# A transformer block on one Trainium2 core: softmax rows normalised in pairs, weight roundings of the output projection moved apart, its first sums in other banks

## The chip, the cores and the metric

The kernel runs on one core of a Trainium2 chip. A core has a matrix engine (TensorE, PE in the profile; PEld is its weight load), VectorE (DVE), ScalarE (ACT), GpSimd (POOL) and SyncE (SP), which here only starts transfers. The engines run side by side, each takes its instructions in order, and they wait for each other through semaphores. Matrix products land in PSUM, of which this kernel uses eight banks of 128 x 512 numbers. Transfers between HBM and the core's memory are issued by SP and POOL into queues and carried out by 16 DMA engines. A special kind, the accumulating load, adds what it reads to what already stands in the tile; it is issued by POOL.

The metric is the device time of one execution in microseconds. Times below are of single executions or medians of several.

## The reference

Inputs are x (512 rows of 1024), weights and gains in float32. The parts that matter here:

```python
q = concat([q_nope, rope(q_rope)]) * (MLA_QK_HEAD ** -0.5)     # 8 heads, 96 wide
s = einsum('qhd,thd->hqt', q, k)                                 # 512 x 512 per head
p = softmax(s); y_mla = p @ v                                  # v is 128 wide per head
merged = sigmoid(z_ma) * y_gla + sigmoid(z_mb) * y_mla         # 512 x 1024
h = h + merged @ w_out                                         # 1024 x 1024
m = rmsnorm(h, g_mlp)
h = h + square(relu(m @ w_ff1)) @ w_ff2                        # 1024 x 4096 x 1024
return rmsnorm(h, g_final)
```

Ahead of them stand a norm, the input projections and a gated linear attention that gives y_gla.

## The kernel before, in words

*Precision.* A float32 operand is split into a high half (rounded on ACT, L93, or with a gain L97) and a low half (the difference, on DVE or POOL, L94 and L98). `mm3` then makes each product from three matmuls: high by high (L88), high by low (L89), low by high (L90). "A rounding step" below is one such pair of ACT and DVE instructions.

*Attention.* It starts at 303.85 us of the profiled span. The 8 heads go in 4 pairs. `up_units(pr)` is a generator that, step by step, loads and splits a pair's weights (wq, wk), and makes its queries (uq), keys (uk) and values (uv). A loop `for n in range(38)` goes over 32 steps of 128 query rows: `att_scores` for row block n (three matmuls into a bank `s`; the negated maximum on DVE, L1007; the exponential with its sum `tot` on ACT, L1010; the reciprocal on DVE, L1011; the scaling, on ACT for even blocks, L1015, and on DVE for odd ones, L1013), `att_flip` for block n - 3 (four transposes into a bank `tp`, L1024, and their rounding into `pT`), and `att_values` for block n - 6 (matmuls into `av`). `merge` multiplies a head's values by its gate on DVE (`tb`, L1052) and adds y_gla on POOL (L1055), which gives `mx` and `my` of the pair. `next(units)` hands one step of the next pair's preparation to the loop in each iteration.

*Output projection.* merged @ w_out is made with seven products in place of eight (m = 1, 2, 5, 6, 3, 7, 4), each of a left operand made of sums of merged blocks and a right operand made of blocks of w_out, B11, B12, B21 and B22. `merged_sums` forms the sums `yo` and `zo` (L928 to L931), `split_sum`, `split_first` and `corner` round them (`ghbo`/`glbo`, `ghco`/`glco`, `gao`, `gdo`). The right side stands in tiles `w2_00` to `w2_31`: `load_w2` fills them through SP's queue (four 256 KB loads for a block), `load_onto` adds another block in place through POOL's queue (two loads of 512 KB, L908), `add_w2` adds two blocks on DVE (L912). `split_part` and `split_w2` round half a block or a block into `bo` and product number, as in bo10 and bo11 (128 x 1024 numbers each). The products land in banks `wox`, `wow` and `woz`, and `add_rows` adds them into the rows `h` (L1298).

*Between projection and feed-forward part.* Each row block of h gets its norm: squares with sums on ACT in two halves (L173), mean and power on DVE and POOL (L180, L183), the scaling in halves on DVE (L1314) and ACT (L1315). PE flips the scaled rows `ms` into banks `mb` (L198), `fm.evacuate` rounds them into `mT`, and `proj_begin`/`proj_run` make the first hidden columns f00 and f01 (`early`), then f02 and so on in four quarters.

*Order.* The Tile framework's scheduler places the instructions. `goes_behind` binds one step behind another on chosen engines. From `begun`, which stands ahead of the projection's products, `in_program_order` keeps PE, DVE and ACT in the order of the code; POOL keeps it from `attending` on, the start of the attention loop. SP's queue takes its loads in the order of the code as far as the scheduler leaves it. PSUM banks are of two kinds, "at" and "mm", four each, handed out in turn: scores, flips and some accumulators take "at"; head preparations, values and others "mm". Rounded weights have 4 buffers for each half, staged ones 3.

Of the kernel before, what the change touches and what calls it, by code (L numbers as in the profile page):

```python
# [56 lines left out]
def tile_block(ctx: ExitStack, tc: tile.TileContext, t, out: bass.AP):  # L57
# [128 lines left out]
    class Flipped:  # L186
# [5 lines left out]
        def rows(self, i, xs):  # L192
            half = i // 2
            if half not in self.banks:
                self.banks[half] = [ps("mm", f"{self.name}b{half}{j}") for j in range(4)]
# [703 lines left out]
    def load_w2(qd, x, w=w2):  # L899
        for g, dst in enumerate(block_tiles(x)):  # L900
            for pp_ in range(2):
                nc.sync.dma_start(dst[:, pp_, :], block_rows(w, qd, x, g, pp_))
# [7 lines left out]
    def add_w2(dst, x, y, op):  # L910
        for g in range(NP // 2):
            nc.vector.tensor_tensor(wq[dst][g], wq[x][g], wq[y][g], op=op)  # L912

# [84 lines left out]
    probs, pTs, avs = {}, {}, {}  # L998

    def att_scores(head, qt):  # L1000
# [8 lines left out]
        tot = sm("tot", 1)  # L1009
        nc.scalar.activation(e, acc, AF.Exp, bias=top, accum_out=tot)  # L1010
        nc.vector.reciprocal(tot, tot)  # L1011
        if qt % 2:
            nc.vector.tensor_scalar(e, e, tot, None, op0=ALU.mult)  # L1013
        else:
            nc.scalar.activation(e, e, AF.Copy, scale=tot)  # L1015
        probs[head, qt] = e
# [225 lines left out]
    units = iter(())  # L1242
    attending = traced()
    sums_of = {}
    for n in range(4 * MH + LAG_C):
        if n % 8 == 1 and n // 8 + 1 < MH // 2:
            units = up_units(n // 8 + 1)
        scored = traced()
        if n < 4 * MH:
            att_scores(n // 4, n % 4)  # L1250
        scored = scored, traced()
        next(units, None)
        b = n - LAG_B
        if 0 <= b < 4 * MH:
            flips = traced()
            att_flip(b // 4, b % 4)
            if b == 0:
                gla_turn(GH - 1, (flips, traced()))

        ready = traced()  # L1260
        if n in (17, 25, 31):
            p = (n - 13) // 8
            y, z = sums_of.pop(p)
            split_sum(wo_left[p], y, 5, 6, f"bo{p}", nc.gpsimd)
            split_sum(wo_left[p], z, 7, 3, f"co{p}", nc.gpsimd)
            if p == 1:
                for p in range(2):
                    split_first(wo_left[p], merged[p][0], f"o{p}", nc.gpsimd)
            goes_behind((ready, traced()), scored, SPLITTERS[:1])
        if n == 20:  # L1270
            load_w2(0, B11, w_out)
            load_w2(0, B21, w_out)
        if n == 24:
            wo_right[1] = split_w2(B11, "bo1")
        if n == 27:
            wo_right[2] = split_w2(B21, "bo2")
        if n == 28:
            load_onto(B11, B12, w_out)
        if n == 30:
            load_w2(0, B12, w_out)  # L1280
            load_w2(0, B22, w_out)
        c = n - LAG_C
# [328 lines left out]
```

## Time and profile before

| what | before |
|---|---|
| three runs | 778.02 (median), 777.01, 778.77 us |
| profiled execution | 777.01 us, its span 775.3 us |
| PE busy | 757.8 us, 98% of the span |
| DVE busy | 584.6 us, 75% |
| ACT busy | 452.9 us, 58% |
| POOL busy | 148.9 us, 19% |
| mean DMA rate | 99 GB/s |
| mean granted clock of PE | 0.99 |

The span runs from the first to the last instruction of the profile. The rows of slices cut it into 40 equal parts of 19.4 us; a digit is the busy share in tenths, and PEclk the clock that TensorE was granted, in tenths of full speed. A row of a group reads: line, engine, operation, output and inputs with their shapes, count; busy microseconds and mean nanoseconds of one; the engine's idle time just before them and what ended it. A row of waits reads: what PE was about to do, on which result of which engine it waited, microseconds in total, times, the longest. The chain of waits goes back from a late instruction, at each step to what released it.

### The profile page before, as it was taken

Reading aid. Unit: us, or ns where it says so; the run is one execution under the profiler, and the core shown is the slowest. Engines: PE = TensorE matmul, PEld = TensorE weight load, DVE = VectorE, ACT = ScalarE, POOL = GpSimd, SP = SyncE. Lnnn points to the kernel's source line nnn. Section 1 sums busy time; section 2 is a strip of 40 time slices with the busy share of each in tenths; the row PEclk is TensorE's granted clock in tenths of the full one; section 3 lists DMA queues with packets and bytes.
Section 4 is the critical chain, followed back from the end, with each engine's and each line's share of the span. In section 5 each row is a group of like instructions: output and inputs, shape, how many; then the busy total and the mean of one; then the engine's idle time right before and its main releaser. Section 6 shows DMA issues by size and latency. Waiting matters only on the chain.

```text
span 775.3 us, 10210 instructions
## 1 busy us (share of the span) xinstructions
PE 757.8 (98%) x3744; PEld 640.1 (83%) x3744; DVE 584.6 (75%) x866; ACT 452.9 (58%) x768; POOL 148.9 (19%) x224
## 2 busy tenths in 40 slices
PE   9999999999999999999799899999999999999996
PEld 7888788889888888898687788888888888888885
DVE  7788999666677776989887677965787578848695
ACT  7556667556475546978735675544644465336644
POOL 0810006161533124044741000000000000000014
PEclk9999999999999999999899899999999999999999
DMA  9734201132325324014766231164106510560002
GB/s 313 244 110 135 71 18 29 54 82 55 82 55 135 52 55 106 22 36 142 219 162 187 84 109 55 58 202 120 55 30 188 151 40 27 171 183 0 28 1 108
DMA packets 94945, 77.09 MB, mean 99 GB/s; under 512 B 15312, under 2 KB 74704, under 8 KB 94896
## 3 DMA queue, kind: packets, MB, share of 16 engines
q1 hardware_dynamic: 92752, 72.24, 31.6%
q0 software_dynamic: 1856, 3.93, 2.7%
q8 instruction: 29, 0.48, 0.3%
q10 hardware_dynamic: 288, 0.28, 0.1%
q14 instruction: 20, 0.16, 0.1%
HBM read 72.76 MB, written 2.10 MB: 97 GB/s over the span
## 4 chain that ended last, share of the span: by engine, by line
PE 93%; DVE 4%; issue 1%; ACT 1%; POOL 0%; POOLq 0%; DVEq 0%; ACTq 0%
PE f L89 8%; PE f L90 8%; PE f L88 8%; PE gx L88 4%; PE gx L89 4%; PE gx L90 4%; PE first L326 3%; PE za L88 2%; PE za L89 2%; PE za L90 2%; PE gz L89 2%; PE gz L90 2%; PE gz L88 2%; PE tp L1024 2%; PE zb L88 1%; PE zb L90 1%
## 5 line engine op out<-in xcount | busy, mean ns | idle before, releaser
L1550 POOL DMA_DIRECT2D gfin<-in_g_final x1 | 0.6, 622 | 283.7 <-PE f L90 283.7
L912 DVE TENSOR_TENSOR w<-w,w 128x1024 f32<-128x1024 f32 x34 | 41.1, 1220 | 0.3
L474 POOL COPY v3f<-rrf 128x4 f32<-128x4 f32 x4 | 2.8, 708 | 135.8 <-DVE rrf L457 135.8
L1010 ACT ACTIVATE e<-s,top 128x512 f32<-128x512 f32 x32 | 21.9, 685 | 6.7 <-DVE top L1007 6.1
L1298 DVE TENSOR_TENSOR h<-h,gx 128x512 f32<-128x512 f32 x32 | 21.5, 680 | 1.9 <-PE gx L90 1.8
L1007 DVE TENSOR_REDUCE top<-s 128x1 f32<-128x512 f32 x32 | 21.6, 679 | 1.4 <-PE s L90 1.4
L94 DVE TENSOR_TENSOR pT<-tp,pT 128x512 fp32r<-128x512 f32 x32 | 21.5, 679 | 0.4 <-ACT pT L93 0.2
L93 ACT ACTIVATE pT<-tp 128x512 fp32r<-128x512 f32 x32 | 18.8, 594 | 4.9 <-PE tp L1024 4.9
L88 PE MATMUL av<-pT,v 128*128 128x256 f32 x64 | 19.5, 304 | 1.3 <-ACT pT L93 1.3
L1024 PE MATMUL tp<-ident,e 128*128 128x128 f32 x128 | 20.1, 281 | 0.0
L89 PE MATMUL av<-pT,v 128*128 128x256 f32 x64 | 18.6, 291 | 0.1
L1024 PEld LDWEIGHTS tp<-ident,e 128*128 128x128 f32 x128 | 16.2, 146 | 3.1 <-issue 0.4
L1370 ACT ACTIVATE fa<-f 128x512 f32<-128x512 f32 x32 | 18.5, 577 | 0.0
L90 PE MATMUL av<-pT,v 128*128 128x256 f32 x64 | 18.4, 288 | 0.0
L93 ACT ACTIVATE ghb<-y 128x512 fp32r<-128x512 f32 x16 | 10.1, 632 | 14.0 <-DVE y L859 14.0
L94 DVE TENSOR_TENSOR sc<-sc,sc 128x512 fp32r<-128x512 f32 x16 | 10.9, 690 | 9.5 <-ACT sc L93 9.5
L88 PE MATMUL s<-kbuf,q 96*128 96x512 f32 x32 | 14.5, 453 | 3.2 <-DVE pT L94 3.2
L93 ACT ACTIVATE sc<-sc 128x512 fp32r<-128x512 f32 x16 | 9.3, 596 | 11.5 <-DVE sc L545 11.5
L1055 POOL TENSOR_TENSOR mx<-tb,za 128x256 f32<-128x256 f32 x8 | 6.9, 868 | 40.9 <-DVE tb L1052 40.9
L93 ACT ACTIVATE b_00h<-w 128x1024 fp32r<-128x1024 f32 x7 | 7.4, 1060 | 12.6 <-PE gx L90 6.0
L93 ACT ACTIVATE b_10h<-w 128x1024 fp32r<-128x1024 f32 x7 | 7.4, 1061 | 12.1 <-PE gz L90 6.0
L93 ACT ACTIVATE b_20h<-w 128x1024 fp32r<-128x1024 f32 x7 | 7.4, 1060 | 11.9 <-PE gz L90 6.0
(1639 smaller groups left out, 2940.7 us busy)
## 6 DMA issues: line engine op xcount, KB each, us to landing
w<-in_w_ff SPq DMA_DIRECT2D x64, 256.0 KB, 3.4
grw<-in_w_in SPq DMA_DIRECT2D x8, 512.0 KB, 8.6
gvw<-in_w_in SPq DMA_DIRECT2D x8, 512.0 KB, 4.8
w<-in_w_out SPq DMA_DIRECT2D x16, 256.0 KB, 5.2
w<-in_w_out POOLq DMA_DIRECT2D x6, 512.0 KB, 7.9
x<-in_xt SPq DMA_DIRECT2D x8, 256.0 KB, 5.3
vw<-in_w_first SPq DMA_DIRECT2D x8, 256.0 KB, 5.4
h<-in_x SPq DMA_DIRECT2D x4, 512.0 KB, 10.7
```

Source lines behind the costliest of these rows:

```text
L88: nc.tensor.matmul(acc, lh, rh, start=start, stop=False, skip_group_check=onto)
L89: nc.tensor.matmul(acc, lh, rl, start=False, stop=False, skip_group_check=onto)
L90: nc.tensor.matmul(acc, ll, rh, start=False, stop=stop, skip_group_check=onto)
L93: nc.scalar.activation(hi, src, AF.Copy)
L94: rest.tensor_tensor(lo, src, raw(hi), op=ALU.subtract)
L326: nc.tensor.matmul(f_accs[i], a[:, i * P : (i + 1) * P], b, start=k == 0 and x == 0, stop=k == KD - 1 and x == 2)
L912: nc.vector.tensor_tensor(wq[dst][g], wq[x][g], wq[y][g], op=op)
L1007: nc.vector.tensor_reduce(top, acc, axis=AX.X, op=ALU.max, negate=True)
L1010: nc.scalar.activation(e, acc, AF.Exp, bias=top, accum_out=tot)
L1024: nc.tensor.transpose(tp[:, k * P : (k + 1) * P], e[:, k * P : (k + 1) * P], ident)
L1298: nc.vector.tensor_tensor(hc, hc, acc, op=op)
L1370: nc.scalar.activation(a, acc, AF.Relu)
```

## The change

Seven things change; the diff has them in the order of the code.

1. *Pairs of rows.* The sums of two row blocks stand in one tile of two columns. A new `att_normalise`, called at even n for blocks n - 2 and n - 1, takes one reciprocal for both, scales the even block on ACT and the odd one on DVE. The scores' steps on ACT and DVE are bound behind those of the flip made two iterations earlier.
2. *Head preparations.* The weights of the next pair are loaded and split earlier (ahead of the loop, at n = 6 and n = 14), and the steps are taken only at n % 8 from 2 to 6.
3. *Rounding of products 1 and 2.* A new `streamed` loads half a block of w_out into a staging buffer (two 256 KB loads on SP) and rounds it, at n = 11 and 13 (B11, product 1) and n = 21 and 23 (B21, product 2). Before, whole blocks were loaded at n = 20 and rounded at n = 24 and 27.
4. *Other blocks.* The tiles of B11 and B21 are then filled for products 5, 6 and 4 by loads and accumulating loads between n = 22 and n = 34, and two additions on DVE for product 6 go. Accumulating loads become 10 from 6, loads of w_out 24 from 16.
5. *Sums of the left side.* `yo` and `zo` of a pair are rounded in iterations of their own (18, 26, 32 and 20, 28, 33), the first blocks at 19, 30 and 35.
6. *Banks.* `wox` and the early f00 and f01 go to "mm", `wow` and the flips of the rows to "at".
7. *Products 3, 7 and 4 with the norms.* `normed` is cut into `second_half_square` and `scaled`; product 4's weights are rounded after both upper rows are scaled; product 7's second half, the flips and their evacuation are interleaved; f00 and f01 begin later; the two lower rows are scaled together after product 4.

```diff
@@ -192,7 +192,7 @@
         def rows(self, i, xs):
             half = i // 2
             if half not in self.banks:
-                self.banks[half] = [ps("mm", f"{self.name}b{half}{j}") for j in range(4)]
+                self.banks[half] = [ps("at", f"{self.name}b{half}{j}") for j in range(4)]
             for k in range(KD):
                 at = (k // 4) * 256 + (i % 2) * P
                 nc.tensor.transpose(
@@ -896,10 +896,11 @@
         c = (x % 2) * S
         return w[r : r + P, c : c + S]
 
-    def load_w2(qd, x, w=w2):
+    def load_w2(qd, x, w=w2, block=None):
+
         for g, dst in enumerate(block_tiles(x)):
             for pp_ in range(2):
-                nc.sync.dma_start(dst[:, pp_, :], block_rows(w, qd, x, g, pp_))
+                nc.sync.dma_start(dst[:, pp_, :], block_rows(w, qd, x if block is None else block, g, pp_))
 
@@ -910,6 +911,15 @@
     def add_w2(dst, x, y, op):
         for g in range(NP // 2):
             nc.vector.tensor_tensor(wq[dst][g], wq[x][g], wq[y][g], op=op)
+
+    def streamed(m, x, g):
+
+        wf = stage(2, S, f"bo{m}{g}")
+        for pp_ in range(2):
+            nc.sync.dma_start(wf[:, pp_, :], block_rows(w_out, 0, x, g, pp_))
+        wh, wl = halves(2, S, f"bo{m}{g}")
+        split(wh, wl, wf)
+        wo_right.setdefault(m, []).append((wh, wl))
 
     def split_part(x, g, name):
         wh, wl = halves(2, S, f"{name}{g}")
@@ -995,7 +1005,7 @@
         for i in range(2):
             heads[2 * pr + i] = (qs[i], kbuf[2 * (pr % 2) + i], vs, slice(i * MV, (i + 1) * MV))
 
-    probs, pTs, avs = {}, {}, {}
+    probs, pTs, avs, tots = {}, {}, {}, {}
 
     def att_scores(head, qt):
         q, kb, _, _ = heads[head]
@@ -1006,14 +1016,17 @@
         top = sm("top", 1)
         nc.vector.tensor_reduce(top, acc, axis=AX.X, op=ALU.max, negate=True)
         e = u2(f"e{head}{qt}")
-        tot = sm("tot", 1)
-        nc.scalar.activation(e, acc, AF.Exp, bias=top, accum_out=tot)
+        if qt % 2 == 0:
+            tots[head] = sm("tot", 2)
+        tot = tots[head]
+        nc.scalar.activation(e, acc, AF.Exp, bias=top, accum_out=tot[:, qt % 2 : qt % 2 + 1])
+        probs[head, qt] = e
+
+    def att_normalise(head, qt):
+        tot, a, b = tots[head], probs[head, qt], probs[head, qt + 1]
         nc.vector.reciprocal(tot, tot)
-        if qt % 2:
-            nc.vector.tensor_scalar(e, e, tot, None, op0=ALU.mult)
-        else:
-            nc.scalar.activation(e, e, AF.Copy, scale=tot)
-        probs[head, qt] = e
+        nc.scalar.activation(a, a, AF.Copy, scale=tot[:, 0:1])
+        nc.vector.tensor_scalar(b, b, tot[:, 1:2], None, op0=ALU.mult)
 
     def att_flip(head, qt):
         e = probs.pop((head, qt))
@@ -1239,51 +1252,69 @@
     rs = gla_squares(h, os)
     gla_gated(h, os, rs)
     LAG_B, LAG_C = 3, 6
-    units = iter(())
+    units = up_units(1)
+    next(units)
     attending = traced()
-    sums_of = {}
+    sums_of, flipping = {}, {}
     for n in range(4 * MH + LAG_C):
-        if n % 8 == 1 and n // 8 + 1 < MH // 2:
-            units = up_units(n // 8 + 1)
+        if n % 2 == 0 and 2 <= n <= 4 * MH:
+            att_normalise((n - 2) // 4, (n - 2) % 4)
         scored = traced()
         if n < 4 * MH:
             att_scores(n // 4, n % 4)
+            if n - 2 in flipping:
+                goes_behind((scored, traced()), flipping[n - 2], SPLITTERS)
         scored = scored, traced()
-        next(units, None)
+        if 2 <= n % 8 < 7:
+            next(units, None)
+        if n in (6, 14):
+            units = up_units(n // 8 + 2)
+            next(units)
         b = n - LAG_B
         if 0 <= b < 4 * MH:
             flips = traced()
             att_flip(b // 4, b % 4)
+            flipping[n] = flips, traced()
             if b == 0:
                 gla_turn(GH - 1, (flips, traced()))
 
-        ready = traced()
-        if n in (17, 25, 31):
-            p = (n - 13) // 8
-            y, z = sums_of.pop(p)
-            split_sum(wo_left[p], y, 5, 6, f"bo{p}", nc.gpsimd)
-            split_sum(wo_left[p], z, 7, 3, f"co{p}", nc.gpsimd)
-            if p == 1:
-                for p in range(2):
-                    split_first(wo_left[p], merged[p][0], f"o{p}", nc.gpsimd)
-            goes_behind((ready, traced()), scored, SPLITTERS[:1])
-        if n == 20:
+        extra = traced()
+        for x, at in (("y", (18, 26, 32)), ("z", (20, 28, 33))):
+            if n in at:
+                p = at.index(n)
+                to = (5, 6) if x == "y" else (7, 3)
+                split_sum(wo_left[p], sums_of[p, x], *to, f"{x}o{p}", nc.gpsimd)
+        if n in (19, 30):
+            p = (19, 30).index(n)
+            split_first(wo_left[p], merged[p][0], f"o{p}", nc.gpsimd)
+        if n < 4 * MH:
+            goes_behind((extra, traced()), scored, SPLITTERS[:1])
+        if n == 35:
+            split_first(wo_left[2], merged[2][0], "o2")
+        if n in (11, 13):
+            streamed(1, B11, (n - 11) // 2)
+        if n in (21, 23):
+            streamed(2, B21, (n - 21) // 2)
+        if n == 22:
             load_w2(0, B11, w_out)
-            load_w2(0, B21, w_out)
-        if n == 24:
-            wo_right[1] = split_w2(B11, "bo1")
+        if n == 23:
+            load_w2(0, B21, w_out, B22)
+        if n == 25:
+            load_onto(B11, B12, w_out)
         if n == 27:
-            wo_right[2] = split_w2(B21, "bo2")
+            load_onto(B21, B11, w_out)
         if n == 28:
-            load_onto(B11, B12, w_out)
-        if n == 30:
             load_w2(0, B12, w_out)
             load_w2(0, B22, w_out)
+        if n == 31:
+            load_onto(B21, B12, w_out)
+        if n == 34:
+            load_onto(B12, B22, w_out)
         c = n - LAG_C
         if c >= 0 and c % 2 == 1:
             att_values(c // 4, (c % 4) // 2)
         if c > 0 and c % 8 == 7 and c // 8 < NP - 1:
-            sums_of[c // 8] = merged_sums(c // 8, nc.gpsimd)
+            sums_of[c // 8, "y"], sums_of[c // 8, "z"] = merged_sums(c // 8, nc.gpsimd)
 
     hrow = []
     for i in range(NT):
@@ -1306,21 +1337,17 @@
 
     span = {}
 
-    def normed(i, last_half):
-        at = traced()
+    def second_half_square(i, c):
+        square_half(hrow[i], c, hparts[i], ms_rows[i], False)
+
+    def scaled(i):
         m = ms_rows[i]
-        square_half(hrow[i], last_half, hparts[i], m, False)
         rs = row_rstd(hparts[i])
         nc.vector.tensor_scalar(m[:, 0:S], hrow[i][:, 0:S], rs, None, op0=ALU.mult)
         nc.scalar.activation(m[:, S:D], hrow[i][:, S:D], AF.Copy, scale=rs)
-        span["norm", i] = at, traced()
 
     def flipped(i):
         fm.rows(i, ms_rows[i])
-        if i % 2 == 1:
-            at = traced()
-            fm.evacuate(i // 2)
-            span["evacuate", i // 2] = at, traced()
 
 
     def prep(m, qd):
@@ -1455,9 +1482,9 @@
 
 
     begun = traced()
-    xs_ = [ps("at", f"wox{rb}") for rb in range(2)]
+    xs_ = [ps("mm", f"wox{rb}") for rb in range(2)]
+    ws_ = [ps("at", f"wow{rb}") for rb in range(2)]
     zs_ = [ps("at", f"woz{rb}") for rb in range(2)]
-    ws_ = [ps("mm", f"wow{rb}") for rb in range(2)]
     wo_accs = {2: ws_, 5: zs_, 3: zs_}
 
     def wo_product(m, rbs=range(2), ps_=range(NP)):
@@ -1471,7 +1498,6 @@
                     m in (1, 2, 5) and p == 0, p == NP - 1, m not in (1, 2, 5))
 
     last = NP - 1
-    split_first(wo_left[2], merged[2][0], "o2", nc.vector)
     g_last = split_first(wo_left[last], merged[last][0], f"o{last}", nc.vector, None, slice(0, HT))
     wo_product(1)
     wo_right[5] = [split_part(B11, 0, "bo5")]
@@ -1479,19 +1505,18 @@
     y, z = merged_sums(last, nc.vector)
     split_sum(wo_left[last], y, 5, 6, f"bo{last}")
     wo_right[5].append(split_part(B11, 1, "bo5"))
-    load_onto(B12, B22, w_out)
-    add_w2(B11, B22, B11, ALU.add)
+    load_w2(0, B11)
     for rb in range(2):
         add_rows(rb, 0, xs_[rb])
     wo_product(2)
-    wo_right[6] = [split_part(B11, 0, "bo6")]
+    wo_right[6] = [split_part(B21, 0, "bo6")]
     for rb in range(2):
         add_rows(rb, 0, ws_[rb])
+    wo_right[6].append(split_part(B21, 1, "bo6"))
+    load_onto(B21, B21, w_out)
+    split_sum(wo_left[last], z, 7, 3, f"co{last}")
+    for rb in range(2):
         first_half_square(rb, 0)
-    wo_right[6].append(split_part(B11, 1, "bo6"))
-    load_onto(B11, B21, w_out)
-    load_w2(0, B21)
-    split_sum(wo_left[last], z, 7, 3, f"co{last}")
     wo_product(5)
     wo_right[3] = [split_part(B22, 0, "bo3")]
     for rb in range(2):
@@ -1511,24 +1536,42 @@
     for rb in range(2):
         wo_product(3, (rb,))
         add_rows(rb, 1, zs_[rb])
-        normed(rb, 1)
-        wo_right.setdefault(4, []).append(split_part(B11, rb, "bo4"))
-    load_w2(0, B11)
-    early = [proj_begin(w1, 0, "f00", "at")]
-    for rb in range(2):
-        wo_product(7, (rb,))
-        add_rows(2 + rb, 1, xs_[rb], ALU.subtract)
-        first_half_square(2 + rb, 1)
-        flipped(rb)
-    early.append(proj_begin(w1, P, "f01", "at"))
-    for rb in range(2):
-        wo_product(4, (rb,))
-        add_rows(2 + rb, 0, xs_[rb])
-        normed(2 + rb, 0)
+        second_half_square(rb, 1)
+        scaled(rb)
+    wo_right[4] = split_w2(B21, "bo4")
+    load_w2(0, B21)
+    wo_product(7, (0,))
+    add_rows(2, 1, xs_[0], ALU.subtract)
+    first_half_square(2, 1)
+    flipped(0)
+    wo_product(7, (1,), range(2))
+    flipped(1)
+    at = traced()
+    fm.evacuate(0, range(4))
+    wo_product(7, (1,), range(2, NP))
+    add_rows(3, 1, xs_[1], ALU.subtract)
+    fm.evacuate(0, range(4, KD))
+    first_half_square(3, 1)
+    span["evacuate", 0] = at, traced()
+    early = [proj_begin(w1, 0, "f00", "mm")]
+    wo_product(4, (0,))
+    add_rows(2, 0, xs_[0])
+    second_half_square(2, 0)
+    early.append(proj_begin(w1, P, "f01", "mm"))
+    wo_product(4, (1,))
+    at = traced()
+    add_rows(3, 0, xs_[1])
+    second_half_square(3, 0)
+    for i in (2, 3):
+        scaled(i)
+    span["norm", 3] = at, traced()
     proj_run(early[0], mT, 0)
     proj_run(early[1], mT, 0, range(5))
     flipped(2)
     flipped(3)
+    at = traced()
+    fm.evacuate(1)
+    span["evacuate", 1] = at, traced()
     proj_run(early[1], mT, 0, range(5, KD))
     for k in range(KD):
         for e in early:
```

## The prediction, made before the result was known

> **What bounds it now.** I read the page's slices first (busy tenths and granted clock), then busy time by stretch, then what TensorE (PE) waited for, then the chain of waits.
>
> ```profile
> PE   9999999999999999999799899999999999999996
> ...
> PEclk9999999999999999999899899999999999999999
> ```
>
> PE is busy in nearly every slice. It dips in two places, around 370 and 430 us, and the granted clock dips with it. The change acts between 304 and 452 us, so I cut that stretch at four PE events: the first attention score (303.85), the end of head 5's scores (360.67), the end of the projection's product 1 (397.01), the middle of its product 3 (416.05) and the first whole product of the feed-forward part (451.67).
>
> ```profile
> core 0: us, PE busy (x) PEld busy (x) DVE busy (x) ACT busy (x) POOL busy (x), PEclk, DMA share, GB/s
> 303.85:360.67 56.82, 56.82 (x375) 50.92 (x374) 50.95 (x103) 47.43 (x106) 16.39 (x22) 1.00 0.26 75
> 360.67:397.01 36.34, 31.67 (x193) 27.53 (x192) 30.75 (x53) 24.82 (x51) 28.10 (x28) 0.91 0.60 176
> 397.01:416.05 19.04, 19.04 (x85) 15.76 (x84) 16.96 (x25) 10.60 (x17) 2.88 (x5) 1.00 0.65 117
> 416.05:451.67 35.62, 31.36 (x190) 27.73 (x189) 22.30 (x40) 19.03 (x39) 2.60 (x6) 0.90 0.40 130
> 375.00:380.00 5.00, 4.38 (x14) 3.58 (x15) 3.60 (x8) 2.65 (x6) 5.00 (x6) 0.50 0.89 290
> 430.00:435.00 5.00, 4.36 (x10) 3.47 (x11) 3.83 (x9) 4.38 (x13) 0.37 (x2) 0.50 0.64 206
> ```
>
> PE is dense in the first and third stretch. In the second it idles 36.34 - 31.67 = 4.67 us (place A), in the fourth 4.26 us (place B). After each idle time it runs at half clock: 4.38 us and 4.36 us of work in the two quoted windows, of which half is lost, 2.2 us each, and some 0.1 us more beyond the window. So A costs 7.0 us and B 6.6 us, 13.6 us in all; no order of the same matmuls saves more here.
>
> ```profile
> PE s L88 <- DVE pT L94: 3.2, 2, 2.7
> PE wox L88 <- DVE h L1298: 3.1, 1, 3.1
> PE av L88 <- ACT pT L93: 1.3, 1, 1.3
> PE mb L198 <- DVE ms L1314: 1.2, 1, 1.2
> ```
>
> At A the releaser is a flipped score tile (pT), late on VectorE (DVE) or ScalarE (ACT). The chain shows why: DVE was busy with rounding steps of the projection's weights (bo), the last stretched to 2.13 us, and a scaling stretched to 1.41 us.
>
> ```profile
> 358.76 0.12 PE av L89
> ...
> 359.64 1.22 DVE bo10l L94
> ...
> 363.26 1.60 DVE bo11l L94
> ...
> 371.43 2.13 DVE bo21l L94
> 373.56 1.41 DVE e L1013
> ```
>
> At B the chain runs through ACT and DVE in turn. The add of product 7 into the rows (h), which frees the accumulator for product 4, stands last, behind bo41l and f00l.
>
> ```profile
> 419.10 0.73 ACT ms L173 x2
> ...
> 420.18 0.58 POOL hp L183
> ...
> 421.41 1.05 ACT bo40h L93
> ...
> 427.63 1.22 DVE bo41l L94
> 428.86 1.14 DVE f00l L94
> 429.99 0.61 DVE h L1298
> ```
>
> **The rounding steps of products 1 and 2.** Four DVE steps of 1.2 us and their ACT halves leave the iterations of heads 6 and 7, where no head preparation is left to feed PE. In the built order they stand beside the scores of heads 1, 2, 4 and 5. DVE was busy 50.95 of 56.82 us in that first stretch; four steps more and some twelve reciprocals fewer (0.155 us each, below) make 53.9 us, 95%. PE stays the longer one, so I cost the move at nothing there. If that cover is gone, each step delays one pT by up to 1.2 us, 4.8 us in all. In the second stretch DVE falls from 30.75 to some 24.5 us, since the four steps took about 6.3 us there.
>
> **Normalising in pairs.** One reciprocal serves two rows, so 16 of 32 go. The price is a wait: an even row's scaling now needs the odd row's sum as well.
>
> ```profile
> L1007 DVE TENSOR_REDUCE top<-s 128x1 f32<-128x512 f32 x32 | 21.6, 679 | 1.4 <-PE s L90 1.4
> ...
> L1011 DVE RECIPROCAL tot<-tot 128x1 f32<-128x1 f32 x32 | 4.9, 155 | 2.6 <-ACT e L1010 2.5
> ...
> L1010 ACT ACTIVATE e<-s,top 128x512 f32<-128x512 f32 x32 | 21.9, 685 | 6.7 <-DVE top L1007 6.1 <-DVE tot L1011 0.4
> ...
> L1015 ACT ACTIVATE e<-e,tot 128x512 f32<-128x512 f32 x16 | 11.5, 717 | 0.3 <-DVE tot L1011 0.3
> L1010 ACT ACTIVATION_READ_ACCUMULATOR e<-s,top 128x1 f32 x32 | 6.4, 200 | 0.0
> ...
> 357.13 0.44 PE tp L1024 x4
> ```
>
> From a score to its flip it is 0.68 (maximum) + 0.69 + 0.20 (exponential and its sum) + 0.16 + 0.72 (scaling) = 2.4 us, about 2.9 with four hand-overs. Against it stands the PE work that the built order puts between the odd score and the even flip. It is least for the last pair: 23 value matmuls of 0.12 us and two flips of 0.44 us, 3.6 us. The other pairs of heads 6 and 7 have 4.1 to 4.9 us, earlier pairs 4.2 to 9. Steps already queued on ACT and DVE (a pT half, a gao half) add up to 1.7 us, so the last pair waits about 1.0 us and one before it 0.4 us. I add 0.5 us for scalings stretched beside POOL's work, as the 1.41 us one was. Ends: nothing, if ACT and DVE run ahead; 1.0 us at each of 16 pairs, if the queues stand full everywhere.
>
> **Extra transfers.** Eight more 256 KB loads go through SP's queue and four more accumulating loads through that of GpSimd (POOL).
>
> ```profile
> L1055 POOL TENSOR_TENSOR mx<-tb,za 128x256 f32<-128x256 f32 x8 | 6.9, 868 | 40.9 <-DVE tb L1052 40.9
> L1055 POOL TENSOR_TENSOR my<-tb,za 128x256 f32<-128x256 f32 x8 | 6.2, 780 | 1.4 <-DVE tb L1052 1.4
> L908 POOL DMA_DIRECT2D w<-in_w_out x4 | 5.0, 1455 | 0.0
> L94 POOL TENSOR_TENSOR glco<-zo,ghco 128x512 fp32r<-128x512 f32 x3 | 4.8, 1602 | 0.0
> L94 POOL TENSOR_TENSOR glbo<-yo,ghbo 128x512 fp32r<-128x512 f32 x3 | 4.2, 1402 | 4.9 <-ACT ghbo L93 4.9
> ```
>
> An issue costs POOL 5.0 / 4 = 1.25 us, so 5 us are added to its 28.10. Behind them stand the low halves of the sums of pair 2 and the merge of heads 6 and 7 (mx, my), which product 1's last quarter needs. From the merge of head 5's second half, the built order has on POOL eight 256-wide steps (0.78 to 0.87 us by the means; 0.73 where nothing disturbs), one 512-wide step of 1.4 us for gao, two issues, and glyo and glzo of 1.4 and 1.6 us; a rounding on ACT and DVE of 0.4 us each follows. That is some 12.3 to 13.7 us; PE has 13.0 us of work there. I take 0.3 us lost at A, ends 0 and 2.5 (the two issues at full length). On SP, f02's weights now wait behind bo21's, with w2 blocks and the rows h after them; all are wanted 15 us or more later. Nothing; ends 0 and 1.5, one such load.
>
> **Banks, order of weight blocks.** The first sums move from the banks of the head preparations to those of scores and flips, and back for wox. The list of waits names no wait for a bank; nothing, ends -0.5 and +0.5 (a hand-over at each). Two additions on DVE (1.2 us each) between products 1 and 2 become accumulating loads, one product earlier. That shortens DVE's 16.96 us of the third stretch, which PE fills anyway, so its worth is at B.
>
> **Product 3 to the feed-forward part.** I walk the built order with the chain's durations, t = 0 at product 3's middle (416.05 before). A row chain (add, square, power, scale) is 3.1 us, and DVE waits it out before the next add. So row 0 is scaled at 3.2, row 1 at 6.1, bo40h and bo41h are done at 8.1, bo41l at 9.5, the add of product 7's first half at 10.1. PE, with product 7 and two sets of flips, gets there at 10.1: 0.1 us lost instead of 3.1. Then come the evacuations of the flips.
>
> ```profile
> 431.86 3.00 ACT L97 ACTIVATE mT<-mb,gvec 128x256 fp32r<-128x256 f32 x8
> ...
> 432.35 3.23 DVE L98 SCALAR_TENSOR_TENSOR mT<-mb,gvec,mT 128x256 fp32r<-128x256 f32 x8 [1.17 <-ACT mT L97]
> ```
>
> Four of them (0.4 us each) stand ahead of the second add of product 7, which ends at 13.6 where PE wanted it at 12.9 (0.7 lost). f00l comes at 16.9 (0.5), f01l, behind the add of product 4 and its square, at 20.5 (0.7), the last two rows' scalings cost 0.45 twice, their evacuation behind f02l 0.6. That is 3.5 us in seven pieces, none over 0.8, where 6.6 stood: 3.1 given back. Ends: all 6.6, or 0.8 if the pieces draw the half clock as before (2.3).
>
> **The sum.** A keeps 1.4 + 0.5 + 0.3 = 2.2 of 7.0 and gives back 4.8. 777.01 - 4.8 - 3.1 = 769.1 us; I say 769. The profiled run took 777.01 us, 1.7 us outside its span of 775.3; the median of the three runs, 778.02, is 1.0 above it.
>
> **Rivals.** *Small stalls keep the clock down.* My stalls at B lie at t = 13 to 27, some within 4 us of each other. One half-clock episode costs 2.3 us: 771.4; both, 773.7. Against it: at A and B the clock was 0.50 only behind waits of which one was 2.7 or 3.1 us long. The Trainium skill (TensorE: Matmul & The Clock Gate, "A second HAM failure mode: psum-queue depth-cycling") says that frequent micro-idles between groups of matmuls make the clock gate swing; by that rule this rival holds.
>
> *All is recovered.* If ACT and DVE run ahead of my walk, PE is dense: 777.0 - 13.6 = 763.4.
>
> *The stall at A only moves.* DVE, at 95% of the first stretch, falls behind the moved steps by 4.8 us, and POOL's issues cost 2.5 in place of 0.3: 769.1 + 4.8 + 2.2 = 776.1, no difference. For it: DVE's narrow room. Against: a DVE busy 90% kept up without a wait.
>
> *Slower: the pair wait.* Each of the 16 pairs holds its even flip for the odd sum, and PE takes flips in order. It decides at (7.9 + 1.4) / 16 = 0.6 us a pair. With 1.0 us each, as I count for the last pair, it is 769.1 + 16 - 1.4 = 783.7. For it: the scheduler gives some early pairs 4.2 us too, and DVE at 95% seldom has an empty queue. Against: most have over 5 us.
>
> **How the numbers follow.** My forecast (766 to 770.5) has 0.56, the clock rival 0.14, all recovered 0.06, moved 0.06, pair wait 0.18. Measurements of this kernel tell about 0.2%, 1.6 us, from no change. Faster: 0.56 + 0.14 + 0.06 = 0.76; same 0.06; slower 0.18. The range goes from the second rival to the moved stall, with 0.4 us above it for the spread of the runs: 763.4 to 776.5. It leaves out the pair wait and little else.
>
> **What would show it.** Right: PE's waits for pT between 361 and 390 are under 0.5 us each but one of about 1 us before the last flips; the clock stays at 1.00; wox waits for h under 1 us; from the first score to product 1's end 88.4 us, from product 3's middle to f02 32.5. Wrong: a clock of 0.50 in any window between 304 and 452; PE waiting for a scaling (e) at most pairs; wox waiting for gao through POOL; bo steps over 1.7 us in their new place.

## The result and the profile after

| | before | changed |
|---|---|---|
| median | 777.58 us (13 runs) | 776.19 us (13 runs) |
| profiled execution | 777.01 us | 775.01 us |

The ratio is 0.9982 (95% interval 0.9974 to 0.9991): faster by 1.4 us (0.2%), where 769 was forecast. The gain at B came; at A one stall went and another took its place. The profiled execution of the changed kernel was the fastest of its 13: its mean granted clock is 0.997, that of the others 0.993 to 0.995, so a typical one loses about 1 us more than the trace shows.

The slices and PE's list of waits, changed kernel:

```profile
PE   9999999999999999999979999999999999999996
...
PEclk9999999999999999999999999999999999999999
```

```profile
PE wox L88 <- ACT gao L93: 5.3, 1, 5.3
...
PE tp L1037 <- ACT e L1028: 0.8, 2, 0.5
PE f L90 <- DVE f01l L94: 0.4, 1, 0.4
...
PE wox L88 <- DVE h L1329: 0.3, 1, 0.3
```

The waits for pT and the long wait for h are gone. One of 5.3 us stands in their place: product 1's last quarter needs gao of the last head pair.

Busy time by stretch, first the changed kernel, cut at the end of as many scores as before (361.32), the start of that wait (390.80), the end of product 1 (398.90), the middle of product 3 (418.18) and the start of f03 (455.13); then the kernel before, to product 1's end and from product 3's middle to f03:

```profile
303.85:361.32 57.47, 57.22 (x376) 51.03 (x375) 52.68 (x93) 49.03 (x107) 17.74 (x24) 1.00 0.26 73
361.32:390.80 29.48, 28.88 (x194) 25.20 (x192) 24.00 (x44) 21.70 (x48) 21.39 (x23) 1.00 0.89 240
390.80:398.90 8.10, 2.79 (x7) 1.99 (x8) 2.11 (x2) 1.36 (x2) 7.68 (x9) 0.82 1.09 259
398.90:418.18 19.28, 19.28 (x86) 15.93 (x84) 17.56 (x26) 11.23 (x18) 4.14 (x6) 0.99 0.98 233
418.18:455.13 36.95, 35.66 (x214) 30.60 (x213) 23.18 (x41) 24.01 (x49) 2.62 (x6) 1.00 0.38 118
```

```profile
303.85:397.01 93.16, 88.49 (x567) 78.45 (x566) 81.70 (x155) 72.25 (x156) 44.49 (x49) 0.96 0.39 114
416.05:457.13 41.08, 36.82 (x213) 32.24 (x212) 26.11 (x46) 23.92 (x49) 2.60 (x6) 0.92 0.43 138
```

Up to 390.80 PE idles 0.25 + 0.60 us only. Then it idles 5.3 us, and its clock is down for some microseconds (mean 0.82 in the third row). Product 1 ends 95.05 us behind 303.85, 1.9 later than before; 0.9 of that is only that the first score began later in this execution (304.74), so the stretch itself took 94.2 us, 1.0 more. From product 3's middle to f03 it is 36.95, 4.1 less. The last column but one tells where to look: the DMA engines were full (0.89 to 1.09) from 361 to 418, where the kernel before had 0.60 and 0.65. (This share adds up the times of the packets, so it can pass 1.)

POOL's timeline of the changed kernel, with what its idle time waited for, and pieces of the chain of waits:

```profile
374.44 2.45 POOL L909 DMA_DIRECT2D w<-in_w_out  x2
...
383.00 1.29 POOL L94 TENSOR_TENSOR gao<-mx,gao 128x512 fp32r<-128x512 f32 x1
386.52 1.20 POOL L909 DMA_DIRECT2D w<-in_w_out  x1 [2.23 <-DMA w<-in_w_out]
391.22 1.20 POOL L909 DMA_DIRECT2D w<-in_w_out  x1 [3.50 <-DMA w<-in_w_out]
391.97 1.75 POOL L94 TENSOR_TENSOR glyo<-yo,ghyo 128x512 fp32r<-128x512 f32 x1
393.20 1.73 POOL L94 TENSOR_TENSOR glzo<-zo,ghzo 128x512 fp32r<-128x512 f32 x1
394.42 1.19 POOL L1068 TENSOR_TENSOR mx<-tb,za 128x256 f32<-128x256 f32 x1
```

```profile
374.44 11.79 DMA w<-in_w_out
...
386.52 1.20 POOL w L909
387.72 3.48 issue
...
394.93 0.69 POOL mx L1068
395.64 0.43 ACT gao L93
396.11 0.79 PE wox L88
```

The changed kernel sums three blocks in the tiles of B21: B22, then B11 onto it (issued at 374.44), then B12 (n = 31). Each of these sums is two loads of 512 KB. Before it may issue the third block's halves, POOL must wait until those of the second have landed, 11.8 and 15.7 us after their issue. It waits at 384 and again at 388, and behind it in its queue stand glyo, glzo and the merge mx; gao is rounded from mx, and PE needs gao.

### The profile page after: what moved, and what is told of

It reads as the page before. It is cut to its first block, busy times and chain, and to the rows that moved or that the text cites. A ratio compares the mean times of both kernels' runs of the same rounds, so it can differ in the third digit from the quotient of the medians.

```text
span 773.3 us, 10231 instructions
## 1 busy us (share of the span) xinstructions
PE 757.3 (98%) x3744; PEld 638.1 (83%) x3744; DVE 579.7 (75%) x848; ACT 453.4 (59%) x768; POOL 152.0 (20%) x228
## 4 chain that ended last, share of the span: by engine, by line
PE 87%; DVE 3%; ACT 3%; POOL 2%; DMA 2%; issue 2%; POOLq 0%; SPq 0%; DVEq 0%; ACTq 0%
PE f L89 7%; PE f L90 7%; PE f L88 7%; PE gx L88 4%; PE gx L89 4%; PE gx L90 4%; PE first L326 3%; PE za L88 2%; PE za L89 2%; PE gz L88 2%; PE za L90 2%; PE gz L89 2%; PE gz L90 2%; DMA w<-in_w_out 2%; PE zb L88 1%
## 5 line engine op out<-in xcount | busy, mean ns | idle before, releaser
L913 DVE TENSOR_TENSOR w<-w,w 128x1024 f32<-128x1024 f32 x32 | 38.7, 1221 | 0.3
L909 POOL DMA_DIRECT2D w<-in_w_out x10 | 12.7, 1454 | 13.5 <-DVE bo60l L94 6.7
L93 ACT ACTIVATE b_00h<-w 128x1024 fp32r<-128x1024 f32 x7 | 7.4, 1059 | 12.3 <-PE gz L90 6.0
```

Source lines behind the costliest of these rows:

```text
L93: nc.scalar.activation(hi, src, AF.Copy)
```

## The experiments

Each run was timed beside the kernel before on the same chip. "To product 1" counts from the run's own first score (303.85 to 304.88 us of its span) to the end of product 1, "B" from product 3's middle to f03. The lag is the time from PE's end of product 3's first half to DVE's start of its add into h.

| run | median us | ratio to before | to product 1 | B | lag |
|---|---|---|---|---|---|
| before | 777.6 to 777.9 | 1 | 93.2 | 41.1 | 2.3 |
| changed | 776.19 | 0.9982 (0.9974 to 0.9991) | 94.2 | 36.95 | 0.2 |
| late_second_add | 776.37 | 0.9985 (0.9974 to 0.9995) | 88.0 | 38.5 | 1.7 |
| rows_before_blocks | 776.14 | 0.9979 (0.9970 to 0.9989) | 94.2 | 36.9 | 0.2 |
| old_3_7_4 | 777.79 | 1.0003 (0.9993 to 1.0013) | 88.0 | 39.9 | 1.7 |
| streamed_alone | 771.10 | 0.9919 (0.9901 to 0.9937) | 87.5 | 40.6 | 2.3 |
| streamed_new_374 | 770.26 | 0.9910 (0.9893 to 0.9926) | 87.4 | 39.3 | 2.3 |
| after_plain_blocks | 771.04 | 0.9922 (0.9908 to 0.9937) | 90.7 | 37.4 | 0.6 |
| plain_blocks_no_pairs | 774.82 | 0.9965 (0.9953 to 0.9977) | 94.9 | 37.4 | 0.7 |
| streamed_accumulated | 778.31 | 1.0012 (1.0003 to 1.0022) | 95.2 | 38.9 | 0.7 |
| swap_adds | 769.35 | 0.9895 (0.9880 to 0.9910) | 88.0 | 38.4 | 1.6 |
| adds_on_pool | 771.17 | 0.9916 (0.9900 to 0.9933) | 87.4 | 40.3 | 3.4 |
| pool_and_pairs | 774.31 | 0.9958 (0.9943 to 0.9973) | 90.4 | 40.3 | 3.4 |
| pool_and_banks | 770.91 | 0.9917 (0.9902 to 0.9931) | 87.3 | 40.1 | 3.4 |

### The new stall: POOL's wait, or full DMA engines

**late_second_add**

```diff
-        if n == 31:
-            load_onto(B21, B12, w_out)
...
+    load_onto(B21, B12, w_out)          # after the loop
```

> The changed kernel with one line moved: the accumulating load of B12 onto B21 is issued after the attention loop in place of n = 31. Theory (order on POOL): the 5.3 us for which PE waits for gao come from POOL standing in that load's wait for the one before it, with glyo, glzo and mx queued behind. Then PE's wait goes, and the half clock after it (about 1.9 us): 776.2 - 7.2 = 769.0 us, no wait of PE over 1 us in 361 to 400. Rival (bandwidth): the DMA engines are full in that stretch, and the gap moves to bo60, which needs the sum in B21: 772 to 775.

The wait for gao went, and product 1 ended 6.1 us earlier, but the whole took 776.37 us. PE's waits and ACT's timeline in this run:

```profile
PE wox L88 <- ACT bo60h L93: 2.1, 1, 2.1
...
PE wox L89 <- DVE bo60l L94: 0.6, 1, 0.6
```

```profile
404.89 1.06 ACT L93 ACTIVATE bo60h<-w 128x1024 fp32r<-128x1024 f32 x1 [8.63 <-issue]
407.69 1.06 ACT L93 ACTIVATE bo61h<-w 128x1024 fp32r<-128x1024 f32 x1 [1.74 <-DMA w<-in_w_out]
```

The rival's mechanism holds here, above its 772 to 775: POOL's order made the first stall, and with that mended the sum in B21 itself is late. (The first row's idle time has no releaser in the profile; the second names the load.) PE then waits at the start of product 6 and again inside it: from product 1's end to product 3's middle it took 25.2 us instead of 19.0, of which 2.7 are idle; the mean granted clock there is 0.86.

**rows_before_blocks**

```diff
-        if n == 28:
-            load_w2(0, B12, w_out)
-            load_w2(0, B22, w_out)
-        if n == 34:
-            load_onto(B12, B22, w_out)
...
+    load_w2(0, B12, w_out)              # behind the loads of h
+    load_w2(0, B22, w_out)
+    load_onto(B12, B22, w_out)
```

> The changed kernel with the loads of B12 and B22 issued behind those of the rows h, and B12's accumulating load after the loop; the load onto B21 stays at n = 31 and still waits on POOL. If the first accumulating load onto B21 lands late (11.8 us) because it shares the DMA engines with these loads, it lands in about 8 us (the median of before was 7.9), POOL is free when gao's low half is done, and the gap nearly goes: 769 to 771. If such a load takes 10 to 12 us by itself, POOL's wait and PE's gap of 5.3 us stay: 776.

No change: the load onto B21 landed just before 386.05, as late as ever, and PE waited 4.3 us for gao and 1.2 us more.

```profile
386.05 1.20 POOL L909 DMA_DIRECT2D w<-in_w_out  x1 [1.97 <-DMA w<-in_w_out]
```

This run does not tell contention from a load that is slow by itself: the rows came earlier and the blocks right behind them, so that the DMA engines were as full from 374 to 386 (busy share 1.08) as in the changed kernel (1.11). The kernel before tells it. It issues two pairs of such loads, at 378.65 beside the loads of h and at 394.67 with the engines nearly free of other loads (plain ones took 0.6% of them from 394.6 to 403). The view of tile w gives the times from issue to landing, the first pair's first:

```profile
DMA to landing us min/median/max: 10.7/12.9/15.1
DMA to landing us min/median/max: 5.6/6.8/7.9
```

Pairs on engines as free took 5.6 to 7.8 us in streamed_alone, after_plain_blocks and adds_on_pool too. The changed kernel's 11.8 and 15.7 us are those of the first kind. So the stall has two conditions: POOL waits for a landing with needed work behind it, and the other loads of that moment about double the time to land. POOL came to the third block 9.8 us behind the issue at 374.44; a pair that landed in 5.6 and 7.9 us would not have held it.

**swap_adds**

```diff
-        if n == 31:
-            load_onto(B21, B12, w_out)
         if n == 34:
-            load_onto(B12, B22, w_out)
+            load_onto(B21, B12, w_out)
...
+    load_onto(B12, B22, w_out)          # after the loop
```

> The changed kernel with two accumulating loads exchanged: B12 onto B21 at n = 34, behind the merge of head 6, and B22 onto B12 after the loop. In late_second_add the four last loads of 512 KB landed within 19.1 us of the first one's issue (388.6 to 407.7), 4.8 us each: they go one after another. If that is the rule, B21 is whole some 10 us after 388.6, bo60 is on time, and neither of the two waits (gao 5.3, bo60 2.7) stands: 768 to 771. If such a load takes as long in any place because the engines are full, bo60 waits again as in late_second_add: 775 to 777.

769.35 us, faster than both kernels. Only the places of two accumulating loads differ from the changed kernel. PE's waits and busy time by stretch:

```profile
PE wox L88 <- DVE h L1328: 1.8, 2, 1.4
...
PE tp L1037 <- ACT e L1028: 0.8, 2, 0.5
```

```profile
303.85:391.88 88.03, 86.64 (x568) 76.71 (x567) 79.06 (x138) 71.92 (x155) 43.77 (x50) 1.00 0.49 137
410.92:449.28 38.36, 35.68 (x213) 30.62 (x212) 24.80 (x43) 23.98 (x49) 2.61 (x6) 1.00 0.47 146
```

The clock is 1.00, and PE waits neither for gao nor for bo60. POOL still waits 1.96 us for a landing, at 389, but the merge of head 6, which product 1's last quarter needs, has been made before. So the loads do not cost by their number; two things decide: what stands behind a load that waits on POOL, and which of two loads goes first, since they land one after another.

**after_plain_blocks** and **streamed_accumulated** take the blocks' handling out of the changed kernel, and put it into a kernel that has nothing else of the change but the streamed weights.

```diff
 # after_plain_blocks, against the changed kernel, in words where lines are left out
-        n = 22 to 34: B21 = B22 + B11 + B12, B11 += B12, B12 += B22 by loads
+        n = 20: load B11; n = 28: load_onto(B11, B12); n = 30: load B12, B22
+    load_onto(B12, B22, w_out)          # after product 1
+    add_w2(B11, B22, B11, ALU.add)
```

> The changed kernel with one part undone: the blocks of w_out are handled as before (B11 by load and one accumulating load, the additions for product 6 on DVE, B21 loaded late); pairs, head preparations, streamed weights, sums, banks and the order of 3, 7 and 4 stay. If the three-block sum by accumulating loads is what cost the gain, the gap of 5.3 us and its half clock go, with nothing in their place: 767 to 769, the prediction's own number. If the pairs or the placement of sums also cost: 770 to 773, with PE waiting for e or gao.

> streamed_alone with the change's handling of the blocks (accumulating loads at n = 25, 27, 31 and 34, no addition on DVE for product 6). If the serial accumulating loads into B21 on POOL's queue are the cause, the loss comes back here, without pairs, banks or new order: 5 to 7 us above streamed_alone, 776 to 778, with PE waiting for gao or bo60. If it takes the changed placement of the sums on POOL as well, it stays at 771 to 772.

Both point the same way: without the three-block sum the changed kernel takes some 5 us less (771.04), with it streamed_alone takes 7.2 us more (778.31, just above the 776 to 778 expected). The wait for gao is back in that run:

```profile
PE wox L88 <- ACT gao L93: 4.0, 1, 4.0
PE wox L88 <- DVE h L1315: 2.9, 1, 2.9
```

after_plain_blocks missed its 767 to 769; its second case held, 770 to 773 with PE waiting for e. PE waited 3.0 us for scalings (e), 2.3 of them once. ACT's timeline there shows that it was in ACT's queue, not in the pair:

```profile
382.92 0.63 ACT L93 ACTIVATE ghyo<-yo 128x512 fp32r<-128x512 f32 x1 [1.66 <-POOL yo L939]
383.45 0.71 ACT L1028 ACTIVATE e<-e,tot 128x512 f32<-128x512 f32 x1
```

ACT stood 1.66 us for a sum that POOL had late, with the scaling queued behind.

### The rounding steps, the pairs, the banks

**streamed_alone** is the kernel before with one part of the change.

```diff
-        if n == 24:
-            wo_right[1] = split_w2(B11, "bo1")
-        if n == 27:
-            wo_right[2] = split_w2(B21, "bo2")
+        if n in (11, 13):
+            streamed(1, B11, (n - 11) // 2)
+        if n in (21, 23):
+            streamed(2, B21, (n - 21) // 2)
```

> The kernel before with one part of the change: the weights of products 1 and 2 staged and rounded at n = 11, 13, 21 and 23; nothing else. If these four rounding steps beside heads 6 and 7 made the stall at A, nearly all of its 7.0 us goes: 771 to 772 from 777.6. Rival (DVE is full in the first stretch without paired reciprocals and earlier head preparation): the stall moves to an earlier head, 776 to 779.

771.10: this part alone is worth 6.8 us by the medians; in the traces product 1 ends 5.7 us sooner after the first score (87.5 against 93.2). The waits at A are gone but for 0.3 us; that of B stays.

```profile
PE wox L88 <- DVE h L1307: 3.1, 1, 3.1
...
PE s L88 <- DVE pT L94: 0.3, 1, 0.3
```

**plain_blocks_no_pairs** and **pool_and_pairs** take the pairs out of after_plain_blocks and put them into adds_on_pool (below).

```diff
-        tot = tots[head]                # two columns, one reciprocal for two rows
+        tot = sm("tot", 1)              # as before, row by row
```

> after_plain_blocks with the rows normalised one by one, as before. The prediction counted 1.4 us for the pairs' wait; the trace of the changed kernel shows 0.8 us of waits for e. If the pairs cost that and give nothing, this run is 0.5 to 1.0 us faster than after_plain_blocks. If DVE needs the 16 reciprocals saved, it is 1 to 2 us slower, with PE waiting for pT.

> adds_on_pool with the rows normalised in pairs. The prediction counted 1.4 us for the pairs' wait: 1 to 1.5 us slower than adds_on_pool, with PE waiting for e. Rival, from plain_blocks_no_pairs (3.8 us slower without pairs): DVE is freed, and it is 0 to 2 us faster.

Both missed. With the old placement of sums, pairs cost 3.1 us (774.31 against 771.17), the way that was expected but twice the size; with the changed placement, taking them away costs 3.8 us, beyond what the rival gave. PE's waits, pool_and_pairs and then plain_blocks_no_pairs:

```profile
PE tp L1036 <- ACT e L1027: 2.6, 3, 1.5
```

```profile
PE tp L1040 <- ACT e L1025: 2.8, 1, 2.8
PE av L88 <- ACT pT L93: 2.1, 1, 2.1
```

In pool_and_pairs ACT has two roundings of the sums (ghbo, ghco) and a pT half between the odd row's exponential and the scaling that PE waits 1.5 us for. In plain_blocks_no_pairs about half of the loss is the clock: behind its two waits it was 0.50 from 388 to 392. So the pair's wait is real, and what it is worth hangs on what else stands in the queues of ACT and DVE. Which part turns the sign was not tried: the two kernels differ among other things in the placement of the sums and of the head preparations, and pool_and_pairs lacks the binding of the scores' steps behind an earlier flip.

**pool_and_banks**

```diff
-    xs_ = [ps("at", f"wox{rb}") for rb in range(2)]
-    ws_ = [ps("mm", f"wow{rb}") for rb in range(2)]
+    xs_ = [ps("mm", f"wox{rb}") for rb in range(2)]
+    ws_ = [ps("at", f"wow{rb}") for rb in range(2)]
```

The flips and the early f00 and f01 change sides with them.

> adds_on_pool with the change's banks: wox, f00 and f01 in mm, wow and the flips of the rows in at. The prediction put the banks at nothing, ends -0.5 and +0.5 us. If the first sums wait for banks of scores and flips, it is slower, with PE waiting for e or pT ahead of wow.

770.91 against 771.17: no difference that the times can tell. The traces below hint at 0.2 us at B.

### Products 3, 7 and 4

**streamed_new_374** has streamed_alone's first part and the change's order of products 3, 7 and 4 (the last hunk of the change, with B11 in place of B21); **old_3_7_4** is late_second_add with the order of before.

> streamed_alone with the change's order of products 3, 7 and 4, norms, flips and evacuations. From product 3's middle to the start of f03 the kernel before took 41.1 us, the changed one 36.95: if the order alone does that, 771.1 - 4.1 = 767.0 us (by the prediction's walk 3.1: 768.0), and the wait of wox for h falls from 3.1 to under 1 us. Rival (the order is worth no more than the 1.4 us between old_3_7_4 and late_second_add, the rest came from DVE's additions being gone): 769.7.

> late_second_add with products 3, 7 and 4, norms, flips and evacuations in the order of the kernel before. If that reordering alone gave back what the trace shows at B (35.6 to 31.5 us), the time is 4.1 us above late_second_add: 773. Rival: B's gain came from the accumulating loads in place of DVE's additions and from the banks; then it is as late_second_add, within 1 us.

770.26 and 777.79: the order was worth 0.8 us (not clear of the spread of the runs) and 1.4 us, not 4.1. The table's last two columns tell why. In the ten kernels with the new order, B is 36.7 to 37.0 us plus DVE's lag (lag 0.2: 36.95; 0.6: 37.4; 1.6: 38.4; 2.3: 39.3; 3.4: 40.3). (The three with the flips and first columns in the old banks have 36.9 to 37.0, the seven others 36.7 to 36.8.) In three with the old order it is 38.2 to 38.3 plus the lag (0.7: 38.9; 1.7: 39.9; 2.3: 40.6), in the kernel before 38.7. So at the same lag the new order gives about 1.5 us. Of the 4.1 us that the changed kernel gains at B, 2.1 are lag; the 0.5 us by which the kernel before lies above the other three is not explained.

Where the lag comes from, the steps for bo61 show, here in streamed_new_374, in the changed kernel and in swap_adds:

```profile
403.65 1.23 DVE L94 TENSOR_TENSOR bo61l<-w,bo61h 128x1024 fp32r<-128x1024 f32 x1 [1.76 <-ACT bo61h L93]
```

```profile
407.60 1.22 DVE L94 TENSOR_TENSOR bo61l<-w,bo61h 128x1024 fp32r<-128x1024 f32 x1
```

```profile
400.49 1.06 ACT L93 ACTIVATE bo61h<-w 128x1024 fp32r<-128x1024 f32 x1 [2.46 <-DMA w<-in_w_out]
```

In the order of before bo61h stands on ACT behind the squares of the rows, DVE waits 1.76 us for it, and two additions of 1.2 us are DVE's as well: lag 2.3. The changed kernel rounds bo61 ahead of the squares (it is in the diff, though not among the seven points) and has no additions: lag 0.2. With only the first of the two, in after_plain_blocks, it is 0.6; with only the second, in streamed_accumulated, 0.7. In swap_adds bo61h waits 2.46 us for the load that now lands late, and the lag is 1.6. PE's stall ahead of it did not give DVE time: at product 1's end DVE was further behind in the changed kernel (bo51l starts 4.0 us after that end) than in streamed_new_374 (2.6 us).

**adds_on_pool** is streamed_new_374 with the two additions on POOL, and was to take the lag off.

```diff
-            nc.vector.tensor_tensor(wq[dst][g], wq[x][g], wq[y][g], op=op)
+            eng.tensor_tensor(wq[dst][g], wq[x][g], wq[y][g], op=op)    # eng: POOL for product 6
```

> streamed_new_374 with the two additions for product 6 on POOL in place of DVE. In streamed_new_374 DVE came to the first add of product 3 2.3 us after PE had made it (413.66 against 411.33), in after_plain_blocks 0.6 us, and that one was 1.9 us shorter from there to f03. If DVE's lag is what holds back the new order's gain, 2.4 us off DVE make it 770.3 - 1.9 = 768.4. If POOL's additions come too late for bo60, or slow DVE down, 770 to 772.

It did the opposite: lag 3.4 us, and 771.17 us, as the second case of the expectation has it. DVE's and POOL's timelines of this run:

```profile
392.10 2.75 DVE L937 TENSOR_TENSOR yo<-my 128x256 f32<-128x256 f32 x1
...
399.29 2.44 DVE L94 TENSOR_TENSOR bo60l<-w,bo60h 128x1024 fp32r<-128x1024 f32 x1
```

```profile
391.94 2.61 POOL L912 TENSOR_TENSOR w<-w,w 128x1024 f32<-128x1024 f32 x1
398.26 2.40 POOL L912 TENSOR_TENSOR w<-w,w 128x1024 f32<-128x1024 f32 x1 [3.71 <-DVE bo51l L94]
```

A DVE step on 256 columns, 0.42 us elsewhere, took 2.75 us, as long as POOL's addition beside it, and bo60l 2.44 in place of 1.22. The two steps lost 3.5 us where two additions of 1.2 us were saved.

## Why the prediction was right or wrong

- **The rounding steps (right).** Moved alone they cost nothing in the first stretch, and nearly all of A's loss went (6.8 us by the medians, 5.7 in the traces, where 7.0 was counted). In the changed kernel PE idles 0.25 us in that stretch. One sign of being wrong came without harm: bo21l took 1.75 us in its new place, in swap_adds too.
- **Extra transfers (this step failed).** I counted an accumulating load on POOL as an issue of 1.25 us: "0.3 us lost at A, ends 0 and 2.5 (the two issues at full length)". The step left out that the third block's loads into B21 wait for the second's to land, and that POOL waits with them. The two waits on POOL were 2.23 and 3.50 us and made PE's 5.3 us; with the half clock after them the stretch to product 1's end took 94.2 us, 1.0 more than before, where 88.4 was forecast. The sign was on my own list: "wox waiting for gao through POOL". A landing at the median of before (7.9 us) would have shown nothing, since POOL came to the third block 9.8 us after the issue; it took the landing beside other loads, 10.7 and 15.1 us in the trace of before, and a walk of POOL's queue with it. (The steps summed there come to 12.7 to 13.9 us without the two roundings, not 12.3 to 13.7; that is small beside the wait.)
- **"The stall at A only moves" (right in time by luck, wrong in cause).** That rival gave 776.1 us with DVE behind by 4.8 us and POOL's issues at 2.5. The loss came through POOL, by a wait and not by issues; DVE was not behind: PE idled 0.25 us in the first stretch and has no wait for pT in its list.
- **The pair's wait.** 1.4 us were counted; the changed kernel shows 0.8 (0.5 the longer of two waits), none of it at the last pair, and pairs cost 3.1 us where the sums stand as before. The rival of 783.7 did not occur.
- **Scalings stretched beside POOL, banks.** No wait in the trace answers to the first (0.5 us counted); in pool_and_banks the banks made no difference that the times can tell.
- **Product 3 to f02 (size nearly right, partly by luck).** 35.6 us became 31.5 in the changed kernel (forecast 32.5), counted to f03 less f02's 5.46 us, since there f02 begins among f00 and f01. The walk let DVE be free at t = 0 and did not ask why. That held in the changed kernel, where bo61 is rounded early and its load had landed; in swap_adds that load is late, DVE was 1.6 us behind, and B gave back 2.7 us against the forecast 3.1. The order of products 3, 7 and 4, which the walk credits, gives some 1.5 us at the same lag. The wait of wox for h, "under 1 us", was 0.3 and 1.8.
- **The clock.** In swap_adds it stayed at 1.00 with stalls of 0.3 to 1.4 us, the longest and the next only 3.3 us apart, while it fell behind the one of 5.3 us. The rival of small stalls did not hold here, and the rule of the Trainium skill cited with it (TensorE: Matmul & The Clock Gate, "A second HAM failure mode: psum-queue depth-cycling") is not seen at this size of stalls. Where between them it turns is not sharp: it fell behind 2.1 and 0.6 us in late_second_add (mean 0.86 over 25 us) and stayed at 1.00 behind 2.3 and 0.8 us in after_plain_blocks.
- **The sum.** With the two loads exchanged, all other parts of the change being there, swap_adds takes 769.35 us (forecast 769.1): 88.0 us to product 1's end (forecast 88.4) and 32.9 from product 3's middle to f02 (38.36 less 5.46; forecast 32.5). That it is so near is partly luck: of the 2.2 us counted as left at A, PE idled 1.4, of which 0.6 was for a merge (tb) that was not counted, and B lost 0.4 more. So the places of these two loads are worth 6.8 us by the medians; in the traces A gains 6.2 by the exchange and B loses 1.4.

## What to carry to other kernels

An issue on an engine's queue is cheap only when it need not wait: for each transfer that is moved or added, ask what it waits for, how long that takes to land beside the other transfers of that moment, and what is queued behind it on the engine that issues it. Two accumulating loads into one tile are a chain of landings, not of issues; put the wanted one first, and behind the work that others wait for. A part's gain read from one trace can belong to other parts: B's 4.1 us were 1.5 of the new order and 2.1 of DVE's lag, and only kernels that differ in one of them told them apart.

## What the runs showed that was not expected

Accumulating loads are heavy on the DMA engines, by the time that their packets take. From 374 to 391 us of the changed kernel, by the DMA view (bytes in MB, share of the 16 engines' time):

```profile
q1 hardware_dynamic: 1139, 2.67, 45.2%
...
q0 software_dynamic: 1043, 2.01, 63.7%
```

q0 carries them: 63.7 / 2.01 = 32% of the engines' time for a MB, against 45.2 / 2.67 = 17% for plain loads. In late_second_add four of 512 KB landed within 19.1 us of the first issue, a mean of 4.8 us each, beside plain loads.

An addition of 2.6 us on POOL held a short DVE step until it was done (2.75 us for 0.42), so moving work from a late DVE to an idle POOL made DVE later. The Trainium skill (GPSIMD Engine Reference, "1. Specifications") says that GpSimd shares its memory interfaces with VectorE and contends with VectorE instructions that have two inputs in SBUF. The step yo<-my has two such inputs, bo60l too, and these rows agree; two adds h<-h,wox beside the second addition, with one of their inputs in PSUM, took 1.27 us together, as they do elsewhere.
